# Mamba mixer of a two-layer trunk: the first input-projection weight is loaded and split ahead of the norm, and the halves of two weights are split in another order

## The chip, the core and the metric

The kernel runs on one core of one Trainium2 chip. The metric is device time in microseconds for one execution of the whole kernel: 2538.79 us, the median of three runs (2536.79 to 2539.12). The profile shows one further execution, which took 2537.33 us; its span from the first to the last instruction is 2535.5 us. Engines are named as in the profile: PE multiplies matrices (PEld is its weight load), DVE and ACT do elementwise work, POOL does a little elementwise work and issues some transfers, SP issues nearly all transfers.

## The reference, cut to what matters

The trunk has two layers over 256 positions of width 2048. Layer 0 mixes tokens by a convolution module, layer 1 by a Mamba-2 mixer; an MLP follows each. The change lies where layer 1 begins: the norm of the residual stream, and the input projection.

```python
u = rmsnorm(h, norm_mix_g[i]) * (1 + sc1) + sh1
mix = mamba2(u, ...)

def mamba2(u, w_in, conv_w, conv_b, dt_bias, a_log, d_skip, norm_g, w_out):
    zxbcdt = u @ w_in                      # 2048 x (z 4096, x 4096, B 1024, C 1024, dt 64)
    xbc = jax.nn.silu(causal_dwconv(xbc, conv_w, conv_b))
    dt = jax.nn.softplus(dt_raw + dt_bias) # the time steps, 64 heads
    A = -jnp.exp(a_log)
    y = ssd_chunked(xs, dt, A, Bm, Cm) + d_skip * xs
    ...
# in ssd_chunked, per chunk of 128 positions
    acum = jnp.cumsum(dtc * a_f, axis=1)
    seg = acum[:, :, None] - acum[:, None, :]
    decay = jnp.exp(jnp.where(tril, seg, -jnp.inf))
```

## The kernel before, in words

**Activations and weights as pairs.** Activations lie transposed, 128 features by 256 positions, 16 such row tiles in all, held as four buffers of four tiles (`u[0]` to `u[3]`). Products are made in a rounded 32-bit format, so each operand is split into a high part and a low part: ACT rounds it (for weights the cast of L387, for activations L538), DVE subtracts (the split's low part, L389 and L539). A weight comes in tiles of 128 x 2048 by one transfer of 1 MB (`load_w`), in a ring of three buffers `w32`, and is split in two halves (`split_half`) into the rings `wh` and `wl`, three buffers each. A matmul with a high weight part covers high and low activations at once, 512 columns; one with a low weight part covers the high activations, 256 columns.

**The norm at the start of layer 1.** The last block of layer 0's MLP adds into the residual (L989), ACT squares each new row tile (L602), PE sums squares over the features (L575), ACT and DVE make the reciprocal root (L581, L582, L549), PE spreads it (L554), and `modulate` makes the 16 row tiles, two at a time: DVE scales (L610), ACT writes the high part (L538), DVE the low part (L539). Everything that PE does in layer 1 waits for these row tiles.

**Time steps and blocks.** `time_steps` multiplies the 64 columns of the time steps (one weight tile `wdt`, 16 matmul groups called kt 0 to 15 below, one for each row tile, L1277 and L1279), then computes softplus, the cumulative sum (a scan, L1314) and exponentials on DVE and ACT, and stores the cumulative sum to memory (`ac_d`) and one exponential (`eac_d`) by POOL transfers. Twenty blocks of 512 columns follow (`block`, matmuls at L418); a block runs over four weight tiles g = 0 to 3, one for each `u[g]`, into four accumulator banks of which six exist. Each bank is emptied through `item`: ACT copies (L1205), DVE adds into `xpad` (L1206), DVE convolves (L1226). After the first blocks a group's `scores` starts: POOL transfers rows of `ac_d` back, spread over the partitions, and DVE adds the causal mask to them (L1360, "the mask add" below).

**What sets the order.** A scheduler places instructions by priority in program order, each engine then runs its own list in order. `high_priority(n)` moves a step n places ahead; `issue_after(x)` keeps an instruction behind x; weight transfers keep program order on SP. In the kernel before, `mamba` makes the row tiles first, then `time_steps` loads and splits `wdt` (its second half's cast waits for the last square, its second half's subtraction for the first four row tiles), and the first block's first weight is split inside `block`, with its low parts held behind `rows`, the last high and low part of `u[0]`:

```python
for blk in range(20):
    self.block(a["win"][blk], u, ..., ahead=None if blk else 0, after=(None, None) if blk else rows)
```

Of the kernel before, what the change touches and what calls it, by code (L numbers as in the profile page):

```python
# [8 lines left out]
F32 = mybir.dt.float32  # L9
F32R = mybir.dt.float32r  # L10
# [5 lines left out]
P = 128  # L16
# [173 lines left out]
class Trunk:  # L190
# [230 lines left out]
    def block(self, src, rhs, evac, pump=None, single=False, ahead=None, after=(None, None)):  # L421
# [5 lines left out]
        for g in range(4):  # L427
            w = self.load_w(src[g])
# [3 lines left out]
            with self.tc.high_priority(self.ahead if ahead is None else ahead):  # L432
                parts = self.split_w(w, (), after if g == 0 else (None, None), after[1] if g == 0 else None)
# [738 lines left out]
    def mamba(self, ss):  # L1172
        nc, a = self.nc, self.a
        self.need(1, SC1, SH1)
        u = []
        with self.tc.high_priority(AHEAD_CHAIN):
            r = self.rstd_bcast(ss, D)
        for g in range(4):
            with self.tc.high_priority(0 if g else AHEAD_CHAIN):
                u.append(self.modulate(r, 1, SC1, SH1, g))  # L1180
            if g == 0:
                rows = self.hi, self.split
        self.time_steps(u, rows)
# [53 lines left out]
        for blk in range(20):  # L1237
            self.block(a["win"][blk], u, lambda j, parts, blk=blk: item(4 * blk + j, parts), ahead=None if blk else 0, after=(None, None) if blk else rows)
# [18 lines left out]
    def time_steps(self, u, first):  # L1257
# [3 lines left out]
        w = self.wp.tile([P, NT, P], F32, tag="w32", name=self.nm("w32"), bufs=3)  # L1261
        self.stream(w, a["wdt"])
        bank = self.bank(self.mm, "mm")
        self.turn_over(bank[:, :P], TO_FIRST, self.pe)
        for i in range(2):
            s8 = slice(8 * i, 8 * i + 8)
            wh = self.wp.tile([P, 8, P], F32R, tag="wh", name=self.nm("wh"), bufs=3)
            wl = self.wp.tile([P, 8, P], F32R, tag="wl", name=self.nm("wl"), bufs=3)
            with self.tc.issue_after(self.sq) if i else nullcontext():
                nc.scalar.copy(out=wh, in_=w[:, s8, :])  # L1270
            with self.tc.issue_after(first[1]) if i else nullcontext():
                nc.vector.tensor_tensor(out=wl, in0=w[:, s8, :], in1=wh.bitcast(F32), op=ALU.subtract)
# [217 lines left out]
```

## Time and profile before

| what | value |
|---|---|
| median of three runs | 2538.79 us (2536.79 to 2539.12) |
| profiled execution | 2537.33 us |
| its span | 2535.5 us |
| busy: PE, DVE, ACT, POOL | 99%, 76%, 52%, 6% of the span |
| chain that ended last, by engine | PE 89%, DVE 5%, DMA 3%, ACT 2% |
| start of layer 1, from 1112 to 1125 us | PE busy 9.61 of 13.00 us |
| from 1125 to 1300 us | PE busy all the time by its rows |

Times in a row of the timeline count from the start of the span. A row gives the start, the length, the engine, the line and what is written from what; a bracket tells how long the engine had been idle before it and which instruction released it. Two matmuls overlap, so a matmul's own length is longer than the step to the next one. A table of stages gives for each stretch of time the busy time of each engine.

### The profile page before, as it was taken

The page shows a single profiled execution, that of the slowest core. Times are in us where ns is not written, and L with a number is a line of the kernel's source. Part 1 is how long each engine was busy: PE and PEld are TensorE (multiplying, and loading weights), DVE is VectorE, ACT ScalarE, POOL GpSimd, SP SyncE. Part 2 cuts the span into 40 slices and gives each one's busy share as a digit, 9 for nine tenths or more (in the row PEclk, how much of TensorE's full clock was granted, in tenths as well). Part 3 has the DMA queues.
Part 4 walks back from the last instruction along what each step waited for, and adds up shares of the span by engine and source line. Part 5 has one row for each costly group of instructions (what it writes and reads, how often), then busy time and mean ns, then how long its engine had stood idle before and what let it go on. Part 6 is the DMA issues. An engine that isn't in the chain of part 4 may idle for free.

```text
span 2535.5 us, 36834 instructions
## 1 busy us (share of the span) xinstructions
PE 2509.7 (99%) x14596; PEld 2166.1 (85%) x14596; DVE 1937.3 (76%) x2524; ACT 1320.2 (52%) x2026; POOL 145.1 (6%) x201
## 2 busy tenths in 40 slices
PE   9999999999999999999999999999999999999998
PEld 7788799988888888888888888888998888888887
DVE  6799888878878888888787878998875565565565
ACT  2088654544434435457777777744454443443444
POOL 0011000000100000001000000000001101001000
PEclk9999999999999999999999999999999999999999
DMA  9998898788888878856555555688765555555554
GB/s 401 420 351 286 343 347 312 281 332 316 321 309 334 322 307 336 311 201 229 199 190 179 171 189 189 254 322 318 288 249 196 194 188 193 189 190 192 193 189 149
DMA packets 94894, 664.31 MB, mean 262 GB/s; under 512 B 10977, under 2 KB 11105, under 8 KB 16769
## 3 DMA queue, kind: packets, MB, share of 16 engines
q1 hardware_dynamic: 89138, 643.82, 68.6%
q0 software_dynamic: 5152, 16.97, 2.4%
q8 instruction: 114, 1.87, 0.3%
q10 hardware_dynamic: 432, 1.19, 0.1%
q14 instruction: 58, 0.48, 0.0%
HBM read 656.50 MB, written 2.20 MB: 260 GB/s over the span
## 4 chain that ended last, share of the span: by engine, by line
PE 89%; DVE 5%; DMA 3%; ACT 2%; issue 1%; SPq 0%; POOL 0%; DVEq 0%; ACTq 0%; POOLq 0%
PE mm L418 49%; PE mm L402 11%; PE mm L460 8%; PE mm L462 8%; PE mm L461 8%; DMA hid<-wmT 2%; DVE taps L693 2%; ACT taps L675 1%; PE mm L797 1%; DVE hid L317 1%; PE ms L1413 1%; DMA wm<-wmT 1%; DVE wm L317 1%; PE ms L797 0%; DVE taps L687 0%
## 5 line engine op out<-in xcount | busy, mean ns | idle before, releaser
L389 DVE TENSOR_TENSOR wl<-w,wh 128x1024 fp32r<-128x1024 f32 x768 | 940.2, 1229 | 474.1 <-ACT wh L387 469.4
L387 ACT CAST wh<-w 128x1024 fp32r<-128x1024 f32 x768 | 806.4, 1051 | 932.2 <-PE mm L418 480.6
L418 PE MATMUL mm<-u,wh 128*128 128x512 f32 x3136 | 994.6, 398 | 0.0
L418 PEld LDWEIGHTS mm<-u,wl 128*128 128x128 f32 x3136 | 587.9, 188 | 139.9 <-DVE wl L389 1.9
L418 PE MATMUL mm<-u,wl 128*128 128x256 f32 x3136 | 617.3, 278 | 1.4 <-DVE wl L389 1.4
L418 PEld LDWEIGHTS mm<-u,wh 128*128 128x128 f32 x3136 | 479.4, 189 | 7.2 <-issue 4.9
L460 PE MATMUL mm<-wh,hid 128*128 128x512 f32 x896 | 350.7, 391 | 0.0
L462 PE MATMUL mm<-wh,hid 128*128 128x512 f32 x896 | 348.7, 389 | 0.0
L461 PE MATMUL mm<-wl,hid 128*128 128x512 f32 x896 | 348.6, 389 | 0.0
L317 DVE SCALAR_TENSOR_TENSOR wm<-wm,scb 128x2048 f32<-128x2048 f32 x134 | 306.2, 2285 | 13.8 <-DMA wm<-wmT 13.7
L402 PE MATMUL mm<-u,wh 128*128 128x256 f32 x1408 | 253.7, 284 | 0.5 <-ACT u L538 0.3
L402 PEld LDWEIGHTS mm<-u,wh 128*128 128x128 f32 x1408 | 218.3, 192 | 3.5 <-ACT u L538 1.3
L461 PEld LDWEIGHTS mm<-wl,hid 128*128 128x128 f32 x896 | 168.2, 188 | 35.5 <-issue 0.5
L462 PEld LDWEIGHTS mm<-wh,hid 128*128 128x128 f32 x896 | 168.2, 188 | 35.4
L460 PEld LDWEIGHTS mm<-wh,hid 128*128 128x128 f32 x896 | 168.2, 188 | 35.1 <-issue 1.0
L402 PE MATMUL mm<-u,wl 128*128 128x256 f32 x704 | 196.1, 283 | 0.3 <-DVE wl L389 0.2
L418 PE MATMUL mm<-hid,wh 128*128 128x512 f32 x448 | 142.0, 398 | 0.0
L402 PEld LDWEIGHTS mm<-u,wl 128*128 128x128 f32 x704 | 133.7, 192 | 0.7 <-DVE wl L389 0.7
L317 DVE SCALAR_TENSOR_TENSOR hid<-hid,scb 128x2048 f32<-128x2048 f32 x46 | 105.2, 2287 | 20.5 <-DMA hid<-wmT 19.8
L675 ACT ACTIVATE taps<-u,par 128x256 f32<-128x256 f32 x248 | 102.4, 500 | 9.1 <-DVE u L665 5.3
L418 PEld LDWEIGHTS mm<-hid,wl 128*128 128x128 f32 x448 | 84.1, 188 | 19.7
L346 POOL TENSOR_TENSOR mod<-mod,par 128x4 f32<-128x4 f32 x40 | 38.9, 972 | 1062.0 <-DVE wm L317 900.5
(263 smaller groups left out, 2191.5 us busy)
## 6 DMA issues: line engine op xcount, KB each, us to landing
w<-w SPq DMA_DIRECT2D x256, 1024.0 KB, 5.0
wm<-wmT SPq DMA_DIRECT2D x139, 1024.0 KB, 7.3
w<-win SPq DMA_DIRECT2D x80, 1024.0 KB, 4.9
hid<-wmT SPq DMA_DIRECT2D x53, 1024.0 KB, 12.3
w<-wout SPq DMA_DIRECT2D x32, 1024.0 KB, 6.9
w<-pw SPq DMA_DIRECT2D x27, 1024.0 KB, 6.0
w<-open SPq DMA_DIRECT2D x16, 1024.0 KB, 14.0
acc<-ac_d POOLq DMA_DIRECT2D x16, 512.0 KB, 8.7
```

The lines of the kernel that those rows point to most:

```text
L317: self.sum = nc.vector.scalar_tensor_tensor(out=w, in0=w, scalar=1.0, in1=self.scb, op0=ALU.mult, op1=ALU.mult, accum_out=m[:, i:i + 1]).ins
L346: nc.gpsimd.tensor_tensor(out=m, in0=m, in1=b, op=ALU.add)
L387: nc.scalar.copy(out=wh, in_=w[:, s, :])
L389: nc.vector.tensor_tensor(out=wl, in0=w[:, s, :], in1=wh.bitcast(F32), op=ALU.subtract)
L402: self.pe = self.nc.tensor.matmul(out, lhsT=lhsT, rhs=rhs, skip_group_check=True, **kw).ins
L418: self.pe = self.nc.tensor.matmul(out, lhsT=lhsT, rhs=rhs, start=start and not lows, stop=stop and bool(lows), skip_group_check=True).ins
L460: mm(banks[q], lhsT=hi, rhs=wh[:, k, :], start=t == 0, stop=False)
L461: mm(banks[q], lhsT=hi, rhs=wl[:, k, :], start=False, stop=False)
L462: mm(banks[q], lhsT=lo, rhs=wh[:, k, :], start=False, stop=t == NT - 1)
L675: st["tap"] = nc.scalar.activation(out=p4[:, q, :], in_=vp[:, k + q:k + q + T], func=AF.Identity, scale=self.col("w_dw", ct * TAPS + k + q ...
L693: nc.vector.tensor_add(wide, wide, products(four("wl"), k))
L797: self.pe = nc.tensor.matmul(o, lhsT=w[:, i, j * P:(j + 1) * P], rhs=u[g][:, t, :], start=ct == 0 and j < 2, stop=ct == NT - 1, skip_group ...
```

## The change

`mamba` now issues the transfers of `wdt` and of the first block's first weight `w`, in this order, before the norm. Ahead of the norm it splits the first half of `wdt` and the first half of `w`; the cast of the latter is free to run at once, its low part stands behind the last addition into the residual (`self.evac`). The second half of `w` stands behind the high and low parts of `u[0]` (cast and subtraction, with the priority of the norm's chain), and the second half of `wdt` behind those of `u[1]`. The first block takes the two halves as given (`there`). Nothing is computed that was not computed before.

```diff
-        return done + [self.split_half(w, 1, *after)]
+        return done if len(done) > 1 else done + [self.split_half(w, 1, *after)]
...
         for g in range(4):
-            w = self.load_w(src[g])
+            w, done = there if there and g == 0 else (self.load_w(src[g]), ())
...
-                parts = self.split_w(w, (), after if g == 0 else (None, None), after[1] if g == 0 else None)
+                parts = self.split_w(w, done, after if g == 0 else (None, None))
...
-        u = []
+        u, rows = [], []
+        wdt = self.wp.tile([P, NT, P], F32, tag="w32", name=self.nm("w32"), bufs=3)
+        self.stream(wdt, a["wdt"])
+        w = self.load_w(a["win"][0][0])
         with self.tc.high_priority(AHEAD_CHAIN):
+            steps = [self.split_steps(wdt, 0)]
+            half = self.split_half(w, 0, None, self.evac)
             r = self.rstd_bcast(ss, D)
         for g in range(4):
             with self.tc.high_priority(0 if g else AHEAD_CHAIN):
                 u.append(self.modulate(r, 1, SC1, SH1, g))
+            rows.append((self.hi, self.split))
             if g == 0:
-                rows = self.hi, self.split
-        self.time_steps(u, rows)
+                with self.tc.high_priority(AHEAD_CHAIN):
+                    halves = [half, self.split_half(w, 1, *rows[0])]
+        steps.append(self.split_steps(wdt, 1, *rows[1]))
+        self.time_steps(u, steps, rows[0])
...
-            self.block(a["win"][blk], u, lambda j, parts, blk=blk: item(4 * blk + j, parts), ahead=None if blk else 0, after=(None, None) if blk else rows)
+            self.block(a["win"][blk], u, lambda j, parts, blk=blk: item(4 * blk + j, parts),
+                       ahead=None if blk else 0,
+                       there=None if blk else (w, halves))
...
+    def split_steps(self, w, i, hi_after=None, lo_after=None):
+        nc = self.nc
+        after = lambda v: self.tc.issue_after(v) if v else nullcontext()
+        s8 = slice(8 * i, 8 * i + 8)
+        wh = self.wp.tile([P, 8, P], F32R, tag="wh", name=self.nm("wh"), bufs=3)
+        wl = self.wp.tile([P, 8, P], F32R, tag="wl", name=self.nm("wl"), bufs=3)
+        with after(hi_after):
+            nc.scalar.copy(out=wh, in_=w[:, s8, :])
+        with after(lo_after):
+            nc.vector.tensor_tensor(out=wl, in0=w[:, s8, :], in1=wh.bitcast(F32), op=ALU.subtract)
+        return wh, wl
```

`time_steps` keeps its matmuls and loses the load and the splits. SP and POOL issue the same things in the same order as before. On PE, DVE and ACT the order differs in the first three blocks and is the same again from the fourth on. In the rows below, which are the engines' lists without times, numbers only tell buffers apart.

On PE at the first row tiles (`wh_9576`, `wl_9577` are the first half of the time steps' weight, `wh_9677`, `wl_9678` that of the block's first weight, `u_9501` is `u[0]`, `u_9518` is `u[1]`) the list before is:

```order
L1277 MATMUL mm_9571<-u_9501,wh_9576 128x512
L1279 MATMUL mm_9571<-u_9501,wl_9577 128x256
L418 MATMUL mm_9674<-u_9501,wh_9677 128x512
L1277 MATMUL mm_9571<-u_9518,wh_9576 128x512
L1279 MATMUL mm_9571<-u_9518,wl_9577 128x256
L1277 MATMUL mm_9571<-u_9518,wh_9576 128x512
L1279 MATMUL mm_9571<-u_9518,wl_9577 128x256
L418 MATMUL mm_9671<-u_9501,wl_9678 128x256 x2
```

and after the change (`wh_9486`, `wl_9487` the time steps, `wh_9490`, `wl_9491` the weight's first half, `wh_9530`, `wl_9531` its second, `u_9513` and `u_9534` the row tiles):

```order
L1291 MATMUL mm_9589<-u_9513,wh_9486 128x512
L1293 MATMUL mm_9589<-u_9513,wl_9487 128x256
L418 MATMUL mm_9683<-u_9513,wh_9490 128x512
L418 MATMUL mm_9683<-u_9513,wl_9491 128x256 x2
L418 MATMUL mm_9684<-u_9513,wh_9490 128x512 x2
L418 MATMUL mm_9684<-u_9513,wl_9491 128x256 x2
L418 MATMUL mm_9681<-u_9513,wh_9530 128x512 x2
L418 MATMUL mm_9681<-u_9513,wl_9531 128x256 x2
L418 MATMUL mm_9682<-u_9513,wh_9530 128x512 x2
L418 MATMUL mm_9682<-u_9513,wl_9531 128x256
L1291 MATMUL mm_9589<-u_9534,wh_9486 128x512
```

The low products of the first half, and most of the second half's products, now stand between the time steps of `u[0]` and those of `u[1]`.

On DVE around the scan of the cumulative sum (`wm` is the time steps' work area, `a` rows are convolutions, `wl` rows are splits) the list before is:

```order
L1226 SCALAR_TENSOR_TENSOR a_9858<-xpad,par,a_9858 128x256
L1309 SCALAR_TENSOR_TENSOR wm_9617<-wm_9617 64x256
L1226 SCALAR_TENSOR_TENSOR a_9858<-xpad,par,a_9858 128x256
L1311 TENSOR_SCALAR wm_9617<-wm_9617,na 64x256
L389 TENSOR_TENSOR wl_9987<-w_1500_9984,wh_9986 128x1024
L1314 SCALAR_TENSOR_TENSOR wm_9617<-ones,wm_9617 64x128 x2
```

and after the change:

```order
L389 TENSOR_TENSOR wl_9987<-w_1500_9984,wh_9986 128x1024
L1320 SCALAR_TENSOR_TENSOR wm_9627<-wm_9627 64x256
L1234 SCALAR_TENSOR_TENSOR a_9858<-xpad,par,a_9858 128x256
L1323 SCALAR_TENSOR_TENSOR wm_9627<-wm_9627 64x256
L389 TENSOR_TENSOR wl_9991<-w_1500_9984,wh_9990 128x1024
L1325 TENSOR_SCALAR wm_9627<-wm_9627,na 64x256
L1234 SCALAR_TENSOR_TENSOR a_9864<-xpad,par,a_9864 128x256
L1328 SCALAR_TENSOR_TENSOR wm_9627<-ones,wm_9627 64x128 x2
```

The scan now stands behind one more weight half of the second block (`wl_9991`); two convolutions have moved ahead of the scan besides (four instead of two since the time steps' sum).

On DVE at the mask adds, before and then after:

```order
L1360 TENSOR_TENSOR acc_9921<-acc_9921,mask 128x1024
L389 TENSOR_TENSOR wl_10037<-w_1505_10030,wh_10036 128x1024
L1360 TENSOR_TENSOR acc_9922<-acc_9922,mask 128x1024
L389 TENSOR_TENSOR wl_10111<-w_1520_10108,wh_10110 128x1024
L389 TENSOR_TENSOR wl_10115<-w_1520_10108,wh_10114 128x1024
L1206 TENSOR_TENSOR xpad<-mm_9887,lo_10065 128x256
```

```order
L389 TENSOR_TENSOR wl_10037<-w_1505_10030,wh_10036 128x1024
L1234 SCALAR_TENSOR_TENSOR a_9876<-xpad,par,a_9876 128x256
L1374 TENSOR_TENSOR acc_9921<-acc_9921,mask 128x1024
L389 TENSOR_TENSOR wl_10111<-w_1520_10108,wh_10110 128x1024
L1374 TENSOR_TENSOR acc_9922<-acc_9922,mask 128x1024
L389 TENSOR_TENSOR wl_10115<-w_1520_10108,wh_10114 128x1024
L1214 TENSOR_TENSOR xpad<-mm_9887,lo_10065 128x256
```

One weight half (`wl_10037`) has moved from behind the first mask add to ahead of it; `mm_9887` is the second block's first accumulator bank, and PE's third block needs that bank again for its third column tile.

More of the change, by code (lines that the diff above doesn't have):

```diff
@@ L1255, in mamba, with time_steps @@
         return st["ss"]
-    def time_steps(self, u, first):
+    def split_steps(self, w, i, hi_after=None, lo_after=None):
[9 more added lines that the diff above has]
+        return wh, wl
+    def time_steps(self, u, steps, first):
         nc, a = self.nc, self.a
         H = HEADS
-        w = self.wp.tile([P, NT, P], F32, tag="w32", name=self.nm("w32"), bufs=3)
-        self.stream(w, a["wdt"])
         bank = self.bank(self.mm, "mm")
         self.turn_over(bank[:, :P], TO_FIRST, self.pe)
[L1265 to L1272, printed above, removed]
+        for i, (wh, wl) in enumerate(steps):
             for k in range(8):
```

2 lines of the change are left out of this document (1 added, 1 removed).

## The prediction, before the run

> **What bounds the kernel now.** I read the page first (busy shares, the chain that ended last), then a table of stages around the start of layer 1, then the timelines of PE, ACT, DVE and POOL there. A difference this kernel can show is about 0.2%, 5.1 us of 2538.8.
>
> ```profile
> span 2535.5 us, 36834 instructions
> PE 89%; DVE 5%; DMA 3%; ACT 2%; issue 1%; SPq 0%; POOL 0%; DVEq 0%; ACTq 0%; POOLq 0%
> ```
> ```profile
> 1117.00:1125.00 8.00, 5.34 (x26) 4.02 (x27) 7.82 (x18) 4.94 (x10) 0.00 (x0) 1.00 0.29 98
> 1125.00:1138.00 13.00, 13.00 (x76) 11.32 (x75) 11.36 (x22) 8.29 (x15) 0.00 (x0) 1.00 0.51 183
> 1138.00:1160.00 22.00, 22.00 (x128) 18.87 (x127) 21.84 (x42) 13.43 (x21) 1.33 (x3) 1.00 0.58 196
> ```
>
> The chain is PE for 89% of the span. After the length the stages give PE, PEld, DVE, ACT and POOL. In the first of them PE works 5.34 of 8.00 us while DVE works 7.82: DVE is the bound there, and only there can the change gain. From 1125 us PE never stops; but from 1138 to 1160 DVE is full as well (21.84 of 22.00). Two engines run in step, and what PE gains ahead of this stage is kept only if DVE follows.
>
> **The waits that go.** PE's timeline, rows with a wait:
>
> ```profile
> 1112.28 1.49 PE L575 MATMUL ms<-ones,sq 128*128 128x1 f32 x12
> ...
> 1116.86 0.91 PE L1277 MATMUL mm<-u,wh 128*128 128x256 f32 x2 [0.35 <-ACT u L538]
> ...
> 1120.39 0.40 PE L418 MATMUL mm<-u,wh 128*128 128x512 f32 x1
> 1121.95 0.50 PE L1277 MATMUL mm<-u,wh 128*128 128x512 f32 x1 [1.17 <-DVE u L539]
> ...
> 1122.69 0.28 PE L1279 MATMUL mm<-u,wl 128*128 128x256 f32 x1
> 1124.32 0.73 PE L418 MATMUL mm<-u,wl 128*128 128x256 f32 x4 [1.35 <-DVE wl L389]
> ```
> ```profile
> 1125.05 0.23 PE mm L1277
> 1125.29 0.12 PE mm L1279
> ```
>
> The chain gives the step from one matmul to the next: 0.23 us for 512 columns, 0.12 for 256. So PE stood from 1120.39 + 0.23 to 1121.95, 1.33 us, and from 1122.69 + 0.12 to 1124.32, 1.51 us, together 2.84. The first wait is for the row tiles of `u[1]`, the second for the low part of the block's first half (DVE, L389). After the change that low part is ready long before: its cast needs the buffer of a half of the MLP's last weight tile. The half before that one was released at 1106.2 (the ACT row of 1106.24 below), a half there is 24 matmuls at 0.12, 2.9 us, so the cast runs from 1109.1 to 1110.2; the subtraction follows the last addition into the residual, ahead of the reciprocal. PE then has as stock, ready or nearly: eight time-step groups at 0.35 = 2.8 us, the first half 8 x 0.23 + 8 x 0.12 = 2.8, the second half 2.8. Both waits go.
>
> **What is late next in the front.** The second half and the time steps' second half are now split inside the row tiles. ACT and DVE before:
>
> ```profile
> 1106.24 1.05 ACT L1270 CAST wh<-w 128x1024 fp32r<-128x1024 f32 x1 [1.77 <-PE mm L402]
> 1110.48 0.42 ACT L602 ACTIVATE sq<-h 128x256 f32<-128x256 f32 x1 [3.19 <-DVE h L989]
> ...
> 1113.02 1.03 ACT L1270 CAST wh<-w 128x1024 fp32r<-128x1024 f32 x1
> 1113.95 0.25 ACT L581 ACTIVATE rcol<-ms,eps 128x2 f32<-128x2 f32 x1
> ...
> 1118.15 0.91 ACT L538 ACTIVATE u<-nrm,mod 128x256 fp32r<-128x256 f32 x2 [0.94 <-DVE nrm L610]
> 1119.08 1.28 ACT L1294 ACT_TABLE_LOAD   x1
> 1120.38 0.20 ACT L1294 ACTIVATE na<-par 64x1 f32<-64x1 f32 x1
> 1120.48 0.89 ACT L538 ACTIVATE u<-nrm,mod 128x256 fp32r<-128x256 f32 x2
> ```
> ```profile
> 1120.28 1.22 DVE L1272 TENSOR_TENSOR wl<-w,wh 128x1024 fp32r<-128x1024 f32 x1
> 1121.42 0.88 DVE L539 SCALAR_TENSOR_TENSOR u<-nrm,mod,u 128x256 fp32r<-128x256 f32 x2
> 1122.21 0.87 DVE L610 SCALAR_TENSOR_TENSOR nrm<-h,mod,ms 128x256 f32<-128x256 f32 x2
> ```
>
> On ACT the new cast stands between the fourth high part and the table load, so the load starts 0.93 later (a cast's step, 1113.02 to 1113.95) and the next high parts at about 1121.35. DVE's pairs take 0.79 each, a split 1.14 (1120.28 to 1121.42). Followed on: high parts 7 and 8 end at 1124.1, the time steps' second cast at 1125.1, the cast of the block's next tile at 1126.1. PE's stock begins at 1116.7, waits 0.5 once, as before, for the first low part, and lasts 8.4 us, to 1125.6: a new wait of 0.5. Its low part comes, behind two pairs, a split and two pairs more on DVE, at 1129.35; PE has 8 highs and two time-step groups meanwhile (2.5 us, to 1128.7): a second wait of 0.65. Besides, the norm's chain loses the cast of L1270 (1113.02) that stood ahead of the root: PE's sums end at 1112.28 + 1.49 = 1113.77, so the root can start at 1113.81, 0.14 sooner. **Front: 2.84 - 1.15 + 0.14 = 1.8 us gained** at about 1130 us.
>
> Costed at nothing: the transfers. SP's list is the same.
>
> ```profile
> 1094.50 0.33 SPq L373 DMA_DIRECT2D w<-wdt  x1
> 1099.98 21.93 SPq L373 DMA_DIRECT2D w<-win  x3
> ...
> 1127.11 0.33 SPq L373 DMA_DIRECT2D w<-win  x1
> ```
> ```profile
> w<-win SPq DMA_DIRECT2D x80, 1024.0 KB, 4.9
> ```
>
> The block's first weight is issued at 1099.98 and lands 4.9 us later, 4 us ahead of its cast. The third `win` tile needs a free buffer, before that of `wdt` (DVE until 1121.50), now that of the first weight (cast to 1120.1, then a split of 1.22, 1121.4): the same. The fourth needs `wdt`, split at about 1126.5, where it had waited until 1127.1. The early cast hides in ACT's idle stretch ahead of the first square (1110.48); without that it would cost its 0.93 on the norm's chain.
>
> **Where the gain meets DVE.** The time steps' sum, the scan and its way through memory:
>
> ```profile
> 1156.50 0.72 DVE L1314 TENSOR_TENSOR_SCAN wm<-ones,wm 64x128 f32<-64x128 f32 x2
> 1157.15 0.45 DVE L1226 SCALAR_TENSOR_TENSOR a<-xpad,par,a 128x256 f32<-128x256 f32 x1
> 1157.53 0.28 DVE L1319 TENSOR_TENSOR wm<-wm 64x128 f32<-64x128 f32 x1
> ```
> ```profile
> 1157.52 0.58 POOL L1324 DMA_DIRECT2D ac_d<-wm  x1 [53.21 <-DVE wm L1314]
> 1158.10 0.54 POOL L1325 DMA_DIRECT2D eac_d<-wm  x1
> 1159.78 1.83 POOL L1354 DMA_DIRECT2D acc<-ac_d  x2 [1.14 <-DMA ac_d<-wm]
> ```
> ```profile
> 1167.70 1.23 DVE L1360 TENSOR_TENSOR acc<-acc,mask 128x1024 f32<-128x1024 f32 x1 [2.83 <-DMA acc<-ac_d]
> 1168.84 1.22 DVE L389 TENSOR_TENSOR wl<-w,wh 128x1024 fp32r<-128x1024 f32 x1
> ...
> 1171.11 2.35 DVE L389 TENSOR_TENSOR wl<-w,wh 128x1024 fp32r<-128x1024 f32 x2
> 1173.38 0.75 DVE L1206 TENSOR_TENSOR xpad<-mm,lo 128x256 f32<-128x256 f32 x2
> ```
> ```profile
> 1170.14 0.47 PE L418 MATMUL mm<-u,wl 128*128 128x256 f32 x2
> ...
> 1173.94 0.65 PE L418 MATMUL mm<-u,wh 128*128 128x512 f32 x2
> ```
>
> The mask add waits 2.83 us for the transfer of `acc`, and behind it on DVE stand a split, the second mask add, two more splits and two evacuations of banks. PE already meets that queue: the pair at 1170.14 takes 0.47 where its neighbours take 0.40, right when the split of 1168.84 ends (1170.06); eleven pairs on, at 1173.94, PE's third block takes the bank that the first `xpad` add frees at 1173.38 + 0.42 = 1173.80. There is 0.1 us of slack, so **PE cannot be 1.8 us early there unless the mask add is**.
>
> When is it? Between the time steps' sum and the scan DVE's list now has the same seven splits but two more convolutions, 0.40 each (1157.15 to 1157.53 is a step): +0.80, in a stretch where DVE is full. The sum itself: PE reaches the last group after eight more block matmuls (4 x 0.23 + 4 x 0.12 = 1.4) and 1.8 sooner, so 0.4 sooner, but one more split (1.14, partly waiting for its cast) stands ahead of it on DVE; I take no shift. For waits on casts, which I can only bound (none, or one cast's 1.05), I take 0.4. So the scan, `ac_d`, `acc` and the mask add come 1.2 us later, with ends of 0 and 2.6 (the latter below). Behind the mask add there are now four long steps instead of five (one split went ahead of it): the first `xpad` add comes at 1173.38 + 1.2 - 1.14, 0.1 us later than before. PE waits for it, loses the 1.8 us, and goes on 0.1 us late. From there the engines' lists agree again within a block, and PE is full to 1300 us and on. **Sum: +0.1 us**, 2537.33 to 2537.4 in the profiled execution's terms; the median of the runs shown lies 1.46 higher, so 2538.9.
>
> **Rivals.**
> - *The gain reaches the end* (0.22): the mask add comes 0.7 us sooner instead of later, because DVE is paced by PE and not by its own list. Then -1.8: 2537.0 at the median. For it speaks that casts wait for PE; against it DVE's 21.84 of 22.00.
> - *Slower: POOL's queue is held by ACT* (0.12). `eac_d` stands ahead of `acc` on POOL and needs the exponential that now waits for two table loads, 2.56 us. It decides once `eac_d` ends on POOL after `ac_d` has landed (1158.64 against 1159.78 before, a slack of 1.1 us). If both loads run behind the scan, `eac_d` is issued at 1158.10 + 1.2 + 2.56 = 1161.9, `acc` at 1162.4 instead of 1159.78, the mask add 2.6 late: 2.6 - 1.14 = +1.4, 2540.2.
> - *A switch of tables costs as much again* (0.02). On ACT the list after the change has two table loads ahead of the exponentials, the convolution's and theirs, where it had none, and two loads more in all. By the rows a switch is 1.28 us and nothing around it: the row ahead ends at 1119.06, the load starts at 1119.08, the next activation at 1120.38. Were ACT to stand as long again at each, the case above would grow by 2.56: 2.6 + 2.6 - 1.14 = +4.1, 2542.9. The Trainium skill, page "ScalarE: Activation LUTs", section "What ACT_TABLE_LOAD costs", says this: 1.28 us for the load and a drain of 1.38 us for every switch, which would make it 2543.1. The trace shows the load as stated and no drain.
> - *A late first weight* (0.01): its cast stands ahead of the squares on ACT, and whatever it waits beyond 1109.4 delays the whole norm one for one. It decides from a landing 9.4 us after issue, against 4.9; only at 15 us would it show, 2544.
>
> **How the numbers follow.** Forecast 0.61, rivals as given, 0.02 for none of these. The forecast's own range: mask add 0 to 2.0 late gives -1.1 to +0.9. All cases but the rare ones lie between -1.8 and +1.4, and the three runs lie up to 2.0 below and 0.3 above their median, of which I allow about 1: 2536.0 to 2541.0. All likely cases are under 5.1 us in size, and even both front waits gone with nothing in their place (2.84 + 0.14) would not pass it: faster 0.03, same 0.93, slower 0.04.
>
> **What would show it.** The first block without the 1.17 and 1.35 us waits, PE's waits of about 0.5 and 0.65 for a cast and a split at 1126 and 1129; the scan near 1158; the mask add near 1169; PE waiting 1 to 2.5 us in all for L389 and for the first `xpad` add between 1169 and 1175. Wrong if the stage from 1160 to 1180 shows PE without a wait, if the mask add comes before 1167.5, or if PE meets a long wait ahead of 1117.

## The result, and the profile after

The changed kernel took 2543.09 us, median of 14 runs (2537.69 to 2545.97); the kernel before took 2537.65, median of 14 (2535.84 to 2539.12). The ratio is 1.0020 with a 95% interval of 1.0013 to 1.0027: 3.3 to 6.9 us slower, where 2538.9, a range of 2536.0 to 2541.0 and "no difference" were forecast, with 0.04 for slower. In a later set of runs the same kernel took 2539.95 (11 runs) beside 2537.74 (27 runs), ratio 1.0010, interval 1.0001 to 1.0019. The loss is real, and its size is 2 to 5 us by the medians. The profiled execution took 2541.91 us, its span 2540.1.

The stages of after; the columns are length, PE, PEld, DVE, ACT and POOL busy, then the granted clock, the DMA share and GB/s.

```profile
1112.00:1117.00 5.00, 4.77 (x24) 4.21 (x24) 2.98 (x9) 1.17 (x3) 0.00 (x0) 0.66 0.00 0
1117.00:1125.00 8.00, 7.96 (x46) 6.79 (x44) 7.31 (x16) 6.88 (x11) 0.00 (x0) 1.00 0.36 133
1125.00:1138.00 13.00, 12.37 (x69) 10.53 (x70) 12.01 (x21) 8.85 (x15) 0.00 (x0) 1.00 0.55 175
1138.00:1160.00 22.00, 22.00 (x127) 18.62 (x126) 21.45 (x43) 14.49 (x22) 0.99 (x2) 1.00 0.63 224
1160.00:1180.00 20.00, 15.04 (x79) 12.96 (x79) 12.80 (x19) 13.88 (x27) 5.88 (x8) 0.87 0.84 244
```

and the last of these stages before the change:

```profile
1160.00:1180.00 20.00, 20.00 (x117) 17.32 (x116) 16.79 (x26) 16.37 (x33) 5.52 (x7) 1.00 0.91 299
```

From 1117 to 1125, PE now works 7.96 of 8.00 us, where it had 5.34: the front did what was forecast. The loss stands in the last row. From 1160 to 1180 PE had worked all 20.00 us before; now it works 15.04, DVE is idle as well, and the clock falls to 0.87. PE's rows with a wait, in the front and there:

```profile
1124.56 0.40 PE L418 MATMUL mm<-u,wl 128*128 128x256 f32 x2
1125.21 1.44 PE L418 MATMUL mm<-u,wh 128*128 128x512 f32 x5 [0.25 <-ACT wh L387]
...
1127.19 0.85 PE L418 MATMUL mm<-u,wh 128*128 128x512 f32 x3
1128.46 0.74 PE L418 MATMUL mm<-u,wl 128*128 128x256 f32 x4 [0.42 <-DVE wl L389]
...
1170.59 0.39 PE L418 MATMUL mm<-u,wl 128*128 128x256 f32 x2
1175.94 1.22 PE L418 MATMUL mm<-u,wh 128*128 128x512 f32 x2 [4.96 <-DVE xpad L1214]
```

One wait of 4.96 us for the first `xpad` addition. DVE, which makes it:

```profile
1110.63 0.48 DVE L989 SCALAR_TENSOR_TENSOR h<-mm,mod,h 128x256 f32<-128x256 f32 x1 [0.23 <-PE mm L402]
...
1160.90 2.35 DVE L389 TENSOR_TENSOR wl<-w,wh 128x1024 fp32r<-128x1024 f32 x2
...
1166.98 1.23 DVE L1374 TENSOR_TENSOR acc<-acc,mask 128x1024 f32<-128x1024 f32 x1 [3.33 <-DMA acc<-ac_d]
1168.12 1.22 DVE L389 TENSOR_TENSOR wl<-w,wh 128x1024 fp32r<-128x1024 f32 x1
1173.19 1.23 DVE L1374 TENSOR_TENSOR acc<-acc,mask 128x1024 f32<-128x1024 f32 x1 [3.85 <-DMA acc<-ac_d]
1174.33 1.22 DVE L389 TENSOR_TENSOR wl<-w,wh 128x1024 fp32r<-128x1024 f32 x1
1175.46 0.75 DVE L1214 TENSOR_TENSOR xpad<-mm,lo 128x256 f32<-128x256 f32 x2
...
1204.25 0.75 DVE L1214 TENSOR_TENSOR xpad<-mm,lo 128x256 f32<-128x256 f32 x2
```

The first mask add waits as it did before. The second waits 3.85 us for its own transfer of `acc`; before, it stood at 1169.97 with no wait at all:

```profile
1169.97 1.22 DVE L1360 TENSOR_TENSOR acc<-acc,mask 128x1024 f32<-128x1024 f32 x1
```

So the second `acc` transfer has become late. It is the second instruction of the last POOL row below, issued about half of 1.84 us after 1161.74, at 1162.7, and it lands at 1173.2, 10.5 us later:

```profile
1157.86 0.58 POOL L1338 DMA_DIRECT2D ac_d<-wm  x1 [55.03 <-DVE wm L1328]
1159.59 0.54 POOL L1339 DMA_DIRECT2D eac_d<-wm  x1 [1.15 <-ACT wm L1335]
1161.74 1.84 POOL L1368 DMA_DIRECT2D acc<-ac_d  x2 [1.61 <-DMA ac_d<-wm]
```

What else moves then? SP's list has the eleventh load of the input projection's weights, the third quarter of its third block (I call it `win[2][2]`, 1 MB). It goes out at 1163.28 in after, and went out at 1170.08 before:

```profile
1163.28 0.33 SPq L373 DMA_DIRECT2D w<-win  x1
```
```profile
1170.08 0.33 SPq L373 DMA_DIRECT2D w<-win  x1
```

Its buffer is that of the weight whose last half is `wl_10037`, the split that the lists ahead of the prediction show moving from behind the first mask add to ahead of it. That split is the second of the DVE row at 1160.90; it now ends at 1163.25 and frees the buffer. Before, the split of 1168.84, behind the first mask add, ended at 1170.06, and the load followed. The queues between 1167 and 1173 us in after (packets, MB, share of the 16 engines' time), `q1` being SP's loads and `q0` POOL's transfers:

```profile
q1 hardware_dynamic: 137, 1.02, 55.8%
q0 software_dynamic: 209, 0.70, 40.8%
```

The load takes more than half of the DMA engines' time while the second `acc` transfer is under way. Such a meeting is not new, it has moved. Before, the tenth load went out at 1160.34, and from 1162 to 1167 SP's queue moved 0.96 MB beside 0.68 MB of POOL's: there it was the first `acc` transfer that had company, 7.9 us from issue to mask add. In after the tenth load goes out at 1156.29, and SP's queue moves only 0.03 MB from 1162 to 1167: the first transfer takes 5.2 us, and the eleventh load meets the second.

To compare executions that start at different times I take, in each, the time from the last addition into the residual (L989) to the end of three steps of the `xpad` additions: the first block's first addition ("1st pair" in the table), the second block's pair (for which PE waits) and the next pair after it. For before these are 36.7, 62.0 and 88.3 us, the latter two from 1112.12, 1173.38 + 0.75 and 1199.68 + 0.75; for after 35.4, 65.6 and 94.4, from the rows above. So after is 1.3 us ahead at the first, 3.6 behind at the second and 6.1 behind at the third, and 6.1 it stays to the end of the span. The same table for all profiles, minus before, in us (those of the experiments are described below):

```
              1st pair  2nd pair  3rd pair   median of runs
after           -1.30     +3.57     +6.06     2543.09
again (after)   -1.95     +2.65     +4.70     2541.19 (one run)
after5 (after)  -1.23     +2.09     +3.63     2539.95
hold            -1.96     -0.80     +1.06     2538.55
table           -1.97     +3.12     +5.77     2542.05
order           -1.97     -2.13     -1.07     2535.66
order5 (order)  -1.95     -2.23     -1.21     2535.41
order_table     -1.97     +2.24     +3.53     2537.77
dummy           -0.01     +2.19     +2.15     2539.79
fill            -1.95     +1.05     +2.76     2540.96
fill_again      -1.96     +3.01     +4.77     2541.89 (one run)
fill5           -1.95     +3.14     +4.91     2540.96
order_before    +1.90     +1.91     +3.51     2539.32
first           -1.98     +1.01     +4.55     2537.14
steps           +2.68     +1.30     +2.62     2539.47
```

In first the instructions around the third pair stand in another order, so that pair is no measure of the end: at the end of the span first is 0.65 us behind before. The medians of the kernel before lay at 2537.65 to 2538.05 in these sets of runs.

### The profile page after: what moved, and what is told of

It is laid out like the page before. It is cut to its first block, busy times and chain, and to the rows that moved or that the text cites. A ratio compares the mean times of both kernels' runs of the same rounds, so it can differ in the third digit from the quotient of the medians.

```text
span 2540.1 us, 36837 instructions
## 1 busy us (share of the span) xinstructions
PE 2512.4 (99%) x14596; PEld 2168.6 (85%) x14596; DVE 1937.2 (76%) x2524; ACT 1327.7 (52%) x2030; POOL 145.2 (6%) x201
## 4 chain that ended last, share of the span: by engine, by line
PE 88%; DVE 5%; DMA 4%; ACT 2%; issue 1%; SPq 0%; POOL 0%; DVEq 0%; ACTq 0%; POOLq 0%
PE mm L418 49%; PE mm L402 11%; PE mm L460 8%; PE mm L462 8%; PE mm L461 8%; DMA hid<-wmT 2%; DVE taps L693 2%; ACT taps L675 1%; DVE hid L317 1%; PE mm L797 1%; PE ms L1427 1%; DMA wm<-wmT 1%; DMA w<-open 1%; DVE wm L317 1%; DMA acc<-ac_d 0%
## 5 line engine op out<-in xcount | busy, mean ns | idle before, releaser
L461 PEld LDWEIGHTS mm<-wl,hid 128*128 128x128 f32 x896 | 168.2, 188 | 35.4 <-issue 0.5
L462 PEld LDWEIGHTS mm<-wh,hid 128*128 128x128 f32 x896 | 168.2, 188 | 35.4
```

What stands on the lines that cost most here:

```text
L461: mm(banks[q], lhsT=hi, rhs=wl[:, k, :], start=False, stop=False)
L462: mm(banks[q], lhsT=lo, rhs=wh[:, k, :], start=False, stop=t == NT - 1)
```

## The experiments

In this part TensorE is PE, VectorE is DVE, ScalarE is ACT, GpSimd is POOL and SyncE is SP. Two theories stood first. **A**: the load of `win[2][2]` meets the second `acc` transfer and delays it; VectorE, which works in order, stands at the second mask add, and the `xpad` additions that TensorE needs stand behind it. **B**, the prediction's own rival: `acc` is issued late, because the scan is later and POOL's queue waits for ScalarE's exponentials and their table loads.

**hold.** The load waits until the second mask add is done (`late` returns that add; the load's buffer gets a one-column fill behind it):

```diff
+        if late:
+            with self.tc.issue_after(late()):
+                self.nc.vector.memset(w[:, 0, :1], 0.0)
         self.stream(w, src)
...
```

> The changed kernel, with the load of win[2][2] held until the second mask add is done (a one-column fill of its buffer by VectorE, queued behind that add, which the load must wait for). Theory A: this 1 MB load, which in the changed kernel goes out at 1163.28 because its buffer is freed ahead of the mask adds, shares the DMA engines with the second acc transfer and makes it land at 1173.2; held back, that transfer lands 6 to 8 us after its issue instead of 10.5, VectorE's wait ahead of the second mask add falls from 3.85 us to under 1, TensorE's wait of 4.96 us for the xpad adds to under 1, no half clock follows it, and the time falls by 5 to 8 us, to 2535.5 to 2538.5. Theory B: the transfer is late because it is issued late (scan later, two more table loads, GpSimd's queue held by the exponentials); the load plays no part, VectorE's wait stays above 3 us and the time above 2541.

DVE and PE:

```profile
1165.53 1.22 DVE L1377 TENSOR_TENSOR acc<-acc,mask 128x1024 f32<-128x1024 f32 x1 [2.59 <-DMA acc<-ac_d]
1166.67 1.22 DVE L392 TENSOR_TENSOR wl<-w,wh 128x1024 fp32r<-128x1024 f32 x1
1168.74 1.23 DVE L1377 TENSOR_TENSOR acc<-acc,mask 128x1024 f32<-128x1024 f32 x1 [0.86 <-DMA acc<-ac_d]
```
```profile
1171.50 0.73 PE L421 MATMUL mm<-u,wh 128*128 128x512 f32 x2 [1.24 <-DVE xpad L1217]
...
1184.43 0.33 PE L1404 MATMUL ms<-ident,wm 128*128 128x128 f32 x1 [1.62 <-ACT wm L1239]
```

2538.55 us (11 runs), ratio 1.0002, interval 0.9993 to 1.0011. The transfer lands 6.85 us after its issue (1161.89 to 1168.74) instead of 10.5, the wait for it falls from 3.85 to 0.86, and TensorE's from 4.96 to 1.24. TensorE's was expected under 1. Little is changed but the load's start (the fill takes VectorE 0.06 us), and that is A: without the load beside it, the transfer is not late. The time stops at that of before, just above what was expected, and the front's 2 us are not kept: 1.24 us go at the `xpad` additions, and the held load now comes late itself.

```profile
1177.84 1.05 ACT L390 CAST wh<-w 128x1024 fp32r<-128x1024 f32 x1 [1.25 <-DMA w<-win]
```

ScalarE stands 1.25 us for it, is late with a SiLU, and TensorE waits 1.62 for that.

**table.** `bT`'s SiLU is queued behind the exponentials, so two table loads go:

```diff
-            nc.scalar.activation(out=dst, in_=y, func=AF.Silu)
+            with self.tc.issue_after(self.eac) if g == 0 and k == 0 else nullcontext():
+                nc.scalar.activation(out=dst, in_=y, func=AF.Silu)
...
```

> The changed kernel, with the first SiLU (of bT) queued on ScalarE behind the two exponentials, so that the two extra table loads go. Theory A (collision of the win[2][2] load with the second acc transfer): acc is issued about 1.3 us earlier and gets by so much more ahead of the load; TensorE's wait falls from 4.96 by 1 to 2 us, it still idles 3 us or more, time 2540 to 2543. Theory B (acc is issued late): the issue of acc goes from 1161.74 to 1159.5 to 1160.5, TensorE's wait falls under 1 us, time 2535.5 to 2538.5.

```profile
1161.18 1.84 POOL L1369 DMA_DIRECT2D acc<-ac_d  x2 [2.02 <-DMA ac_d<-wm]
```
```profile
1175.76 1.22 PE L418 MATMUL mm<-u,wh 128*128 128x512 f32 x2 [5.05 <-DVE xpad L1214]
```

2542.05 us (11 runs), ratio 1.0015, interval 1.0007 to 1.0024. `acc` is issued 0.56 us earlier in the span, or 0.84 measured from the last residual addition (1110.91 here, 1110.63 in after), and only 0.25 against again, the second profile of the changed kernel below (50.27 us behind that addition here, 50.52 there). A expected 1.3; POOL now waits longer for `ac_d` to land. TensorE's wait is not shorter, where A expected 1 to 2 us less. B falls as the cause as far as ScalarE's table loads go: without the two of them `acc` goes out hardly earlier, and TensorE waits as long.

**order.** The load stays where it is, and the second mask add is queued behind the two `xpad` additions (and the weight split between them):

```diff
-            with self.tc.issue_after(c["mark"]):
+            with self.tc.issue_after(self.xadd if g == 0 and q else c["mark"]):
...
```

> The changed kernel, with the second mask add queued on VectorE behind the two xpad adds of block 1 and one weight split, for which TensorE waits. The second acc transfer stays late by either theory (VectorE still waits 1 to 3 us for it). If the price comes through VectorE's queue alone, as theories A and B both say, TensorE's wait falls under 1.5 us, no half clock follows, time 2536 to 2539. If TensorE would have stopped for the split behind the second mask add anyway, the wait only moves by some 2 us: time 2540 to 2543.

```profile
1169.27 1.23 DVE L389 TENSOR_TENSOR wl<-w,wh 128x1024 fp32r<-128x1024 f32 x1 [0.28 <-ACT wh L387]
1170.41 0.75 DVE L1214 TENSOR_TENSOR xpad<-mm,lo 128x256 f32<-128x256 f32 x2
1172.12 1.23 DVE L1374 TENSOR_TENSOR acc<-acc,mask 128x1024 f32<-128x1024 f32 x1 [0.96 <-DMA acc<-ac_d]
```
```profile
1160.00:1180.00 20.00, 20.00 (x118) 17.47 (x118) 15.73 (x23) 18.29 (x34) 5.85 (x8) 1.00 0.88 272
```

2535.66 us (11 runs), ratio 0.9991, interval 0.9983 to 1.0000, just under what was expected. The transfer is late as before (issued at 1162.5, used at 1172.1, 9.7 us), yet TensorE works 20.00 of 20.00 us. So the collision by itself does not stop TensorE. It does because the mask add stood on VectorE ahead of work that TensorE needs. That sharpens A: collision and queue order are both needed. Half of the front's gain is lost all the same: 2.13 us ahead at the second pair, 1.07 at the third, with a wait of 0.84 us for a SiLU on ScalarE at 1182.67 between them.

**dummy.** Is a 1 MB load over `acc` enough in the kernel before? A copy of 1 MB is added on SP's queue behind the load of the quarter before (`extra` is an unused DRAM buffer, given for the third block alone):

```diff
             w = self.load_w(src[g])
+            if extra is not None and g == 1:
+                self.stream(extra, src[g])
...
```

> The kernel before, with a copy of 1 MB (win[2][1] again, from DRAM into an unused DRAM buffer) on SyncE's queue behind the load of win[2][1], so that it runs while acc arrives, as the win[2][2] load does in the changed kernel. Theory A: the first or second acc transfer lands 2 to 4 us later, VectorE stands that much longer ahead of a mask add, TensorE stops for the xpad adds, time 2 to 7 us above before: 2540 to 2545. Theory B: a transfer more over acc costs under 1 us: 2537 to 2539.

```profile
1168.79 1.23 DVE L1363 TENSOR_TENSOR acc<-acc,mask 128x1024 f32<-128x1024 f32 x1 [5.05 <-DMA acc<-ac_d]
```
```profile
1171.20 0.51 PE L418 MATMUL mm<-u,wl 128*128 128x256 f32 x2 [1.99 <-DVE wl L389]
```

2539.79 us (11 runs), ratio 1.0007, interval 0.9998 to 1.0016. VectorE waits 5.05 us instead of 2.83 ahead of the first mask add, 2.2 more, TensorE stops for 1.99 us, and the second pair is 2.19 us late: the low end of the waits that A expected, and a time just under its 2540. The ratio's interval reaches below 1, so this run rests on its profile. It is the first transfer that is hit here, since the copy runs earlier than the load does in after.

**fill, fill_again, after5 and fill5: what does the half clock cost?** The trace's clock record shows full clock in the profile of before until 2529 us. In after it falls to a half for 6.83 us, from 1174.65 on, 3.7 us after TensorE stops (1175.94 - 4.96 = 1170.98). Sixteen matmuls on constants go where TensorE stops, in the third block ahead of its third column tile:

```diff
+                    if fill and (g, i, j) == (0, 0, 2):
+                        self.pe = self.turn_over(self.bank(self.ms, "ms")[:, :P], fill, self.pe)
...
```

> The changed kernel, with 16 matmuls on constants into an unused bank put on TensorE's queue where it stops at 1170.8, so that it is busy for some 3.7 us of its 5 us wait. The wait itself stays. If the half clock that follows the wait (6.83 us, in which a step of four matmuls took 1.28 us instead of 0.70) sets the pace there, it goes away and the time falls by 2.5 to 3.5 us, to 2539 to 2541. If VectorE and ScalarE, with their work heaped up behind the late mask add, set the pace in that stretch, the time stays at 2542 to 2544.

The first set gave 2540.96 us (10 runs), 2.1 us under after's 2543.09 of another set. But the profile showed 1.71 us lost behind the wait (+1.05 to +2.76), at full clock. A second profile followed.

> The kernel of the run named fill once more, for a profile of a second execution. If the half clock after the wait sets the pace there, TensorE falls back by 1 us less or more in the stretch behind the wait (up to the third xpad pair after the change) than the 2.5 us of the changed kernel, with its wait alike. If it does not, it falls back by 2.5 us again, at full clock.

Its TensorE rows behind the stop, with no half clock in that stretch:

```profile
1176.68 0.73 PE L418 MATMUL mm<-u,wh 128*128 128x512 f32 x2 [1.48 <-DVE xpad L1216]
...
1184.62 0.73 PE L418 MATMUL mm<-u,wh 128*128 128x512 f32 x2 [0.69 <-ACT wh L387]
...
1185.87 0.50 PE L418 MATMUL mm<-u,wl 128*128 128x256 f32 x2 [0.52 <-DVE wl L389]
```

It falls back by 1.76 us, between the two cases. At full clock TensorE runs into ScalarE and VectorE, which carry the work left by the late mask add. Both kernels side by side:

> The changed kernel, timed beside fill5 and order5 on one chip. As before: 2541 to 2544, 3 to 5.5 us above the kernel before.

> The kernel of the run named fill (16 matmuls on constants where TensorE stops), beside the changed kernel on one chip. If the half clock behind the wait sets the pace, 2 to 3.5 us below it. If ScalarE and VectorE set the pace there, as the profiles of again and fill_again say (2.06 and 1.76 us lost in that stretch), 0.3 to 1 us below it.

2539.95 and 2540.96 us (11 runs each): the changed kernel lies 1 us below what was expected, and the fill gains nothing; it lies 1 us above the changed kernel, where either case had it below. Between the second and the third pair the three profiles of after lose 2.49, 2.05 and 1.54 us with 6.83, 6.83 and 3.41 us at half clock; the three with the fill lose 1.71, 1.76 and 1.77 at full clock. The half clock adds 0.8 us at most here (2.49 - 1.71). The first set's 2.1 us was a difference between two sets of runs.

**again.** The changed kernel, a second profile:

> The changed kernel once more, for a second profile of it. By theory A the order of the issues sets the collision, so it comes in every execution: the load of win[2][2] goes out within 3 us of acc, the second acc transfer lands 9.5 us or more after its issue, TensorE waits 4 to 5.5 us for the xpad adds. If the loss came of the half clock at 1113 to 1116 in front, which one profile showed, the wait varies with it, and without it is 2 us or less.

```profile
1172.90 1.23 DVE L1374 TENSOR_TENSOR acc<-acc,mask 128x1024 f32<-128x1024 f32 x1 [3.83 <-DMA acc<-ac_d]
```
```profile
1175.65 1.22 PE L418 MATMUL mm<-u,wh 128*128 128x512 f32 x2 [4.68 <-DVE xpad L1214]
```

2541.19 us. The load goes out at 1163.27, the second transfer takes 10.2 us, TensorE waits 4.68 us, and there is no half clock in front. So the collision repeats, and the front's half clock is no part of it. In after5 the transfer took 8.9 us and TensorE waited 3.40: its size varies, and with it the time.

**first.** One part alone: the first weight early, the time steps' second half as before.

```diff
-        steps.append(self.split_steps(wdt, 1, *rows[1]))
+        steps.append(self.split_steps(wdt, 1, self.sq, rows[0][1]))
```

> One part of the change alone: the first block's first weight is loaded and split ahead of the norm; the time steps' second half is cast behind the last square and split behind the first row tile, as in the kernel before. The wait of 1.35 us for this weight's split goes, that of 1.17 us for the second row tiles stays, so some 1.3 us are gained in front. In this kernel's order the two xpad adds stand ahead of the second mask add on VectorE, so theory A (TensorE pays for the late transfer through VectorE's queue) expects no stop at 1170 and 2535.5 to 2537.5. If the collision of the transfers or ScalarE's two more table loads cost by themselves, it is 2539 or more.

2537.14 us (10 runs), ratio 1.0000, interval 0.9991 to 1.0010: within what A expected, but no gain. TensorE works 7.94 of 8.00 us from 1117 to 1125, so it has the whole of the front's gain (1.98 us at the first pair, 1.95 in again), more than I expected of it, and loses it again in waits of 0.67 and 1.31 us further on (at 1173.52 and 1180.01). The scheduler moved much else in this kernel (`acc` is issued 5 us later), so it supports A only weakly.

**steps.** The other part alone; the first weight is loaded and split in its block again:

```diff
-        w = self.load_w(a["win"][0][0])
...
-            half = self.split_half(w, 0, None, self.evac)
...
-                       there=None if blk else (w, halves))
+                       after=(None, None) if blk else rows[0])
```

> The other part alone: the time steps' second half is cast and split behind the second row tiles; the first weight is loaded and split as in the kernel before. The wait of 1.17 us for the second row tiles goes, some 1 us is gained in front. The split that frees win[2][2]'s buffer stands behind the first mask add, as in the kernel before, so theory A expects that load to go out too late to meet the second acc transfer, no stop, and 2535.5 to 2538. If an earlier front alone brings the loss, whatever the order at the mask adds, it is 2540 or more.

2539.47 us (10 runs), ratio 1.0007, interval 0.9998 to 1.0017, between the two cases: my expectation of a gain in front was wrong, for the first pair is 2.68 us late.

```profile
1117.81 0.50 PE L1286 MATMUL mm<-u,wh 128*128 128x512 f32 x1 [0.84 <-DVE u L539]
...
1120.12 0.50 PE L1286 MATMUL mm<-u,wh 128*128 128x512 f32 x1 [1.30 <-DVE u L539]
...
1121.98 0.66 PE L1286 MATMUL mm<-u,wh 128*128 128x512 f32 x1 [0.84 <-DVE u L539]
```

Without the first weight's products TensorE has nothing to do between the row tiles and waits three times; in this profile the clock stood at a half for 3.41 us besides, from 1122.15. So the gain in front comes with the first weight's early split, and the other part alone loses. At the mask adds there is no stop, as A expected.

**order_before.** The kernel before, with order's edit:

> The kernel before, with the second mask add queued behind the two xpad adds, as in the run named order. If order's gain (2535.66 beside 2537.80) is the front's 1.8 us, which reach the end once VectorE's queue no longer holds TensorE, this kernel, without the front's gain, takes as long as before: 2537 to 2538.8. If the order by itself is worth the 2 us, it takes 2535 to 2536.3.

2539.32 us (10 runs), ratio 1.0004, interval 0.9995 to 1.0014: no gain, and 0.5 us above the upper end of what was expected. In this kernel the second mask add falls further back on VectorE than in order, so the two differ a little; but as far as it goes, the order is worth something only behind the earlier front. Its profile also shows that the front of the kernel before can be throttled:

```profile
1112.00:1117.00 5.00, 4.63 (x22) 4.08 (x22) 2.79 (x8) 2.37 (x6) 0.00 (x0) 0.66 0.00 0
1117.00:1125.00 8.00, 5.60 (x25) 4.37 (x24) 7.48 (x16) 5.13 (x9) 0.00 (x0) 0.90 0.38 133
```

**order_table.** Both edits, to see whether order can be bettered:

> The changed kernel with both edits: the second mask add behind the xpad adds (order), and bT's SiLU behind the two exponentials (table), which takes two table loads of 1.28 us from ScalarE. In order TensorE still waited 0.84 us at 1182 for a SiLU on ScalarE. If ScalarE's backlog is of these loads, that wait goes and the time is 2534.5 to 2535.4; if it is of the table loads between the exponentials of acc and the SiLUs from 1174 on, which stay, it is as order: 2535.4 to 2536.2.

```profile
1170.81 1.23 DVE L1375 TENSOR_TENSOR acc<-acc,mask 128x1024 f32<-128x1024 f32 x1 [6.96 <-DMA acc<-ac_d]
```
```profile
1173.23 0.51 PE L418 MATMUL mm<-u,wl 128*128 128x256 f32 x2 [3.40 <-DVE wl L389]
```

2537.77 us (10 runs), above either expectation. The load goes out at 1162.44, 0.8 us earlier than in order, and here the first transfer is hit: the first mask add waits 6.96 us, and nothing in order's edit lets the split pass that one. Why the first transfer and not the second was late in this profile is open.

**order5.** Order once more, beside after5 and fill5:

> The kernel of the run named order (second mask add behind the two xpad adds), beside both on one chip. If the 2.1 us below the kernel before are real: 2535 to 2536.5, and 5 to 8 us below the changed kernel. If they were a chance of that chip, 2537 or more.

2535.41 us (11 runs), ratio 0.9994, interval 0.9986 to 1.0003; 4.5 us under after5, where 5 to 8 were expected. Order lay under the kernel before by 2.1 and 2.3 us in the medians of two sets, while the intervals reach 1.0000 and 1.0003: the best of these kernels, by some 0.1%, at the edge of what can be told. The granted clock, on record for every execution, says where part of it comes from. It is 0.999 in the profiles of before, hold, order and order5, which show no half clock ahead of the kernel's last 10 us. Executions of the kernel before at 0.999 took 2536.2 us on average (8 of 33, beside order) and 2536.1 (5 of 27, beside order5); those of order at 0.999 took 2535.6 (10 of 11) and 2535.2 (8 of 11). So at the same clock order is 0.6 to 1.0 us ahead, in line with the 1.07 and 1.21 us that the profiles show at the third pair, and the rest of the 2 us goes with the lower clock of most executions of the kernel before.

## Why the prediction was wrong, point by point

- **What bounds the kernel now: right.** DVE bounds the front, and what PE gains there is kept only if DVE follows.
- **The waits that go: right.** Both are gone, and the early cast cost the norm nothing: PE's first product of the row tiles comes 4.60 us after the last residual addition (again, hold, order), 4.74 before, the 0.14 sooner that was forecast.
- **What is late next in the front: right.** There are new waits for a cast and a split, forecast at 0.5 and 0.65 us. Counted as there, from the end of the last step, they are 0.41 (1124.56 + 0.24 to 1125.21) and 0.58 (1127.19 + 0.69 to 1128.46); the brackets, which leave out the overlap, give 0.25 and 0.42. The gain at the first pair is 1.95 us at full clock (again, fill, order5), forecast 1.8. In the profile of after it is 1.30, since there the clock stood at a half for 3.41 us in front.
- **Costed at nothing, the transfers: the first step that failed.** I followed SP's list to the fourth `win` load and left it there as unchanged. Seven loads on, one goes out 6.8 us earlier in the span (5.3 measured from the last residual addition), over `acc`.
- **Where the gain meets DVE: where the number went wrong.** The scan and the first mask add came close to the forecast: after runs 1.49 us earlier in its span (1110.63 against 1112.12), so the scan at 1156.84 is 1158.3 in before's times (forecast near 1158), and the mask add at 1166.98 is 1168.5 (forecast near 1169). The failed sentence is "four long steps instead of five (one split went ahead of it)". I counted the 1.14 us of VectorE that the split takes, and not the buffer that it frees. And I let the second mask add follow the first at once, as it had, without asking whether its own transfer would still be there: +0.1 us was forecast at the first of these `xpad` additions, +3.6 measured in the profile, and PE waits 4.96 us where 1 to 2.5 were named.
- **From there PE "goes on 0.1 us late": wrong by 1.5 to 2.5 us.** Behind the stop ScalarE and VectorE carry a backlog, and TensorE falls back by that much again up to the third pair, with or without the half clock.
- **The rivals.** "The gain reaches the end" (0.22) is not this kernel; order comes halfway to it, with 1.07 and 1.21 of 1.97 us kept once VectorE's queue no longer holds TensorE. "POOL's queue is held by ACT" had its outcome, but not by its mechanism: `acc` is issued at 1163.2 in before's times against 1159.78, 3.5 us late, more than the rival's 2.6. By the rival's own condition the exponential did not decide, for `eac_d` was done on POOL at 1160.13, and POOL then stood 1.61 us more for `ac_d`, which landed 3.9 us after its issue (2.3 before). From 1158 to 1161 the tenth load moved 0.92 MB beside it; that the load delayed `ac_d` too is likely, but no run tests it. Nor did the late issue decide the mask add: the first transfer then took 5.2 us instead of 7.9, and table shows no gain. "A switch of tables costs as much again" fell: in the ACT rows of after below the activation follows the load at once, and these rows show no drain. No rival was a collision of transfers, and that was the case.

```profile
1157.39 1.28 ACT L1332 ACT_TABLE_LOAD   x1
1158.68 0.41 ACT L1332 ACTIVATE wm<-wm 64x128 f32<-64x128 f32 x1
```

- **"All likely cases are under 5.1 us": the chances failed with it.** A stop of several us was not in my list of cases, so slower got 0.04. The interval, 3.3 to 6.9 us, lies across that bound.
- **The clock gate was left out.** The prediction has no term for it. After a stop of 5 us it did set in. The Trainium skill, page "TensorE: Matmul & The Clock Gate", section "HAM oscillation — how this bites in real kernels", says that a wait of over some 3.4 us lets the array fall to half clock; in after it fell 3.7 us into the stop, but in again 2.4 us into it, and in after5 0.4 us behind the end of a stop of 3.40, so the length of the stop alone does not set the moment here. By the page's rule that half of the throttled time is lost, 6.83 us would cost 3.4, an estimate; the profiles of after beside those with the fill say 0.8 or less, and with the fill TensorE waits for ScalarE and VectorE in that stretch at full clock too.

Settled by the runs: the load makes the second transfer late (hold, again), and TensorE pays because the mask add stands ahead of the `xpad` additions (order). Not settled: why the transfer takes 8.9 us in one execution of the changed kernel and 10.5 in another, and where the kernel before is throttled in the executions with a lower clock (the profile of order_before shows it in the front; the profile of before shows none).

## What to carry to other kernels

When a change moves a step that is the last reader of a buffer, follow the buffer: name the load that it releases, when it now goes out, and which other transfer is on the DMA engines then. An engine that works in order should not stand at a wait for a transfer ahead of work that the bounding engine needs; with the wait behind that work, the same collision did not stop it. And time the parts alone as well as together: here one part alone had the whole gain in front, the other alone lost, and what reached the end hung on an order on VectorE that neither part set.

## What the runs showed of the hardware

Two queues share the DMA engines, so a short transfer stretches with what runs beside it. In hold, with no load beside it, POOL's queue moved 1.32 MB in 6 us (1162.5 to 1168.5, the row below); in after it moved 0.70 MB in 6 us (1167 to 1173) beside 1.02 MB of the load.

```profile
q0 software_dynamic: 376, 1.32, 67.6%
```

The Trainium skill, page "DMA: Bandwidth & Descriptors", section "Queues, rings and completion order", says that each engine goes round its queues packet by packet; the two queues do move side by side here, but no run shows the single turns.

The half clock came in steps of 3.41 us, and not in every execution: in front in after and after5 but not in again, and twice in the front of order_before, where the first pair came 1.90 us late. In the front of after it set in at 1113.21, with no idle stretch of TensorE over 0.3 us in the 3.41 us ahead of it, but with 16 matmuls of one column. The Trainium skill, page "TensorE: Matmul & The Clock Gate", section "What's actually happening", says that the window is 3413 ns and runs free of the kernel, so that its phase differs from run to run; the traces agree, with the half clock behind the stop setting in at 1174.65, 1173.37 and 1175.32 in the three profiles of the changed kernel.
